# A last expert pair in a half and two quarters of its columns, and stores of whole tiles

## Chip, cores and metric

One core of one Trainium2 chip. The metric is the device time of one execution in microseconds, a median of runs; less is better. TensorE does the matmuls, VectorE and ScalarE the work on whole rows, GpSimd a few products, and SyncE (SP) issues the transfers.

## What is computed

Two layers of a transformer on 512 latent tokens of width 1024 (256 more tokens are context): layer 0 mixes by attention, layer 1 by pooling over windows of tokens. Each layer ends in a mixture of experts, 32 experts in 4 groups, two per token, and the whole in a norm:

```python
x_lat = x_lat + g_m * o_l                       # the layer's mixer
tokens = modulate(rms_norm(x_lat, norm_ffn_g[i]), sh_f, sc_f)
# per expert e and its tokens:
gu = h_pad[rows] @ w_gu[e]
y  = (silu(gu[:, :512]) * gu[:, 512:]) @ w_down[e]
f  = zeros.at[row_tok].add(y * row_w)
x_lat = x_lat + g_f * f
...
return rms_norm(x_lat, final_norm_g)
```

All of it is float32; a product that feeds the residual stream is split into a high and a low part of a shorter format and summed from both.

## The kernel before, in words

The residual stream x lies on chip as four tiles of 128 tokens by 1024 columns, `self.x(j)`, two of them side by side in each of the two tiles `self.xt`. The experts are worked through in 16 pairs: tokens of a pair are gathered by a one-hot product (line 1335), multiplied by the gate and up weights (1358), turned (1370), multiplied by the down weights (1383), weighted (1396), split into a high part on ScalarE (1397) and a low part on VectorE (1391), and scattered back to the tokens by a second one-hot product into PSUM tiles pc (1412), which VectorE adds to x (1414). The products of one pair run while the additions of the pair before are done.

The last pair of a layer has no later pair to hide its additions. `last_down` (1418) does it by halves of the 1024 columns. Each down tile holds half of the rows for 512 columns, so a half needs two tiles, `st.get()`. The order is written out by hand, and each engine works through its own instructions in the order in which they are written:

```python
products(0, 0); products(0, 1); parted(0); products(1, 0)
added(0)
after()
products(1, 1); parted(1)
...
added(1, then)
```

`products` (1431) makes a half of y in PSUM, `parted` weights and splits it (1396, 1397, 1437), `added` sums the four token tiles (1443), first all four high parts and then all four low parts, adds them to x (1446) and squares the result on ScalarE with a sum along the row (1447). From the two sums of squares comes the reciprocal root of the next norm, for two token tiles at a time (`rstd_steps`, 474 to 481): a small VectorE instruction, a root on ScalarE, and five small VectorE instructions. `after` is empty in layer 0; in layer 1 it is `gained` (1824), four products of x's first half by the final gain on GpSimd.

`last_down` is used twice. In layer 0 its norms go to the pool layer: four normed tiles xn, on VectorE, ScalarE, VectorE and GpSimd (1647, 1649), which TensorE turns (1674) and which are summed over windows; between these TensorE makes the modulation products ada_ps (354). In layer 1 the norms go to `final` (1826): ScalarE scales the first half of a token tile (1830), VectorE the second (1831), and each half is stored by its own transfer (1833).

All weights come through one stream of transfers on SP (118), in a fixed order. A tile's slot is one of 22, which the large working tiles (`self.big`, y and o among them) share; a slot is handed on when the tile's last reader is done, and `st.done()` lets the next transfer be written into the program.

Of the kernel before, what the change touches and what calls it, by code (L numbers as in the profile page):

```python
# [11 lines left out]
F32 = mybir.dt.float32  # L12
F32R = mybir.dt.float32r
BF16 = mybir.dt.bfloat16
I32 = mybir.dt.int32
AF = mybir.ActivationFunctionType
ALU = mybir.AluOpType
# [3 lines left out]
D = 1024  # L21
KD = D // 128
SEQ = 512
NT = SEQ // 128
# [154 lines left out]
class Kernel:  # L179
# [1238 lines left out]
    def last_down(self, aT, w, gf, inv, after):  # L1418


        nc, mp, pm, st = self.nc, self.mp, self.pm, self.st
        ss = [self.sm.tile([128, NT], F32, name=f"sq{h}") for h in range(2)]
        P = self.scatter(inv)
        py = [pm.tile([128, 512], F32, tag="y", name="py") for _ in range(2)]
        y = [self.big([128, 2, 512], F32R, "y") for _ in range(2)]

        def products(h, q):
            wd = st.get()
            for j in range(2):
                for e in range(2):  # L1430
                    nc.tensor.matmul(py[h][64 * e:64 * e + 64], aT[:, 2 * q + j, 64 * e:64 * e + 64], wd[:, e, j],  # L1431
                                     start=(q + j == 0), stop=(q + j == 2), tile_position=(0, 64 * e))
            st.done()

        def parted(h):
            self.gated(py[h], w, gf, h, y[h])
            nc.vector.tensor_tensor(y[h][:, 1], py[h], y[h][:, 0].bitcast(F32), op=ALU.subtract)

        def added(h, then=None):
            ps = [pm.tile([128, 512], F32, tag=t, name="pc") for t in ("c", "g", "c", "u")]  # L1440
            for part in range(2):
                for j in range(NT):
                    nc.tensor.matmul(ps[j], P[:, j * 128:(j + 1) * 128], y[h][:, part], start=(part == 0), stop=(part == 1))  # L1443
            for j in range(NT):
                xs = self.x(j)[:, h * 512:(h + 1) * 512]
                nc.vector.tensor_add(xs, xs, ps[j])  # L1446
                nc.scalar.activation(mp.tile([128, 512], F32, name="act"), xs, AF.Square, accum_out=ss[h][:, j:j + 1])  # L1447
                if then:
                    then(j)

        products(0, 0)
        products(0, 1)
        parted(0)
        products(1, 0)
        added(0)
        after()
        products(1, 1)
        parted(1)
        nc.vector.tensor_scalar(ss[0], ss[0], 1.0 / D, EPS, op0=ALU.mult, op1=ALU.add)
        r = [self.sm.tile([128, 2], F32, name=f"nr{z}") for z in range(2)]  # L1460
        steps = [self.rstd_steps(r[z], ss[1][:, 2 * z:2 * z + 2], ss[0][:, 2 * z:2 * z + 2], f"n{z}") for z in range(2)]

        def then(j):
            if j == 2:
                next(steps[0])

        added(1, then)

        def norms():

            next(steps[0])
            next(steps[1])
            for z in range(2):
                if z:
                    next(steps[1])
                for j in range(2):
                    yield 2 * z + j, r[z][:, j:j + 1]

        return norms()

    def overflow(self, i, gf):
# [344 lines left out]
    def final(self, norms):  # L1826
        nc = self.nc
        for j, r in norms:
            o = [self.big([128, 512], F32, "o") for _ in range(2)]
            nc.scalar.activation(o[0], self.xg[j], AF.Copy, scale=r)  # L1830
            nc.vector.scalar_tensor_tensor(o[1], self.x(j)[:, 512:], r, self.gn[:, 512:], op0=ALU.mult, op1=ALU.mult)  # L1831
            for h in range(2):
                nc.sync.dma_start(self.out[j * 128:(j + 1) * 128, h * 512:(h + 1) * 512], o[h])


# [36 lines left out]
```

## Time and profile before

| | before |
|---|---|
| median of 3 runs | 1404.93 us (1404.92 to 1408.68) |
| the profiled execution's own time | 1406.14 us |
| its span | 1404.2 us |
| TensorE, weight loads beside it | 94%, 53% of the span |
| VectorE, ScalarE, GpSimd | 48%, 26%, 11% |
| read from memory | 472.06 MB, 338 GB/s over the span |
| TensorE's granted clock, mean | 0.974 |

The profiler took one execution. A row gives an engine's instructions with their start and busy time; an idle time in brackets stands ahead of the instruction that ended it, with the instruction that released it. A traced float32 matmul stands for half of one in the program, so 12 of the program are 24 in the trace. Durations are sums of a stretch where rows are merged ("x4"): the end of the last less the start of the first.

### The profile page before, as it was taken

How to read it: one execution, taken by the hardware profiler on the slowest of the kernel's cores; microseconds unless marked ns; L12 is line 12 of the kernel's file. 1: busy time of each engine (PE TensorE's matmuls, PEld its weight loads, DVE VectorE, ACT ScalarE, POOL GpSimd, SP SyncE). 2: the span in 40 equal slices, each digit the busy share in tenths (PEclk: the TensorE clock that was granted, in tenths of full speed). 3: DMA queues.
4: the chain of work that ended last, by engine and by line, in shares of the span. 5: the costliest groups of instructions: out<-in, count | busy, mean ns of one | idle time of the engine just before them, and what ended most of it. 6: DMA issues, size and time to landing. Idle time of an engine off the chain costs nothing. (4 is left out here: it accounts for less than half of the span.)

```text
span 1404.2 us, 18564 instructions
## 1 busy us (share of the span) xinstructions
PE 1320.3 (94%) x7134; PEld 741.4 (53%) x7135; DVE 672.1 (48%) x1288; ACT 367.4 (26%) x707; POOL 153.7 (11%) x142
## 2 busy tenths in 40 slices
PE   4799999999799999999999997789999999999995
PEld 1588677778544544455444444654445544455432
DVE  2777788767723433243333437632433433343325
ACT  2454678753211111111111114511111111111103
POOL 1523253430000000000000014200000000000001
PEclk8899999999899999999999999889999999999998
DMA  9412845178489999999999999358999999999994
GB/s 379 153 61 65 355 152 179 52 249 325 162 344 428 426 427 426 426 427 426 426 427 426 421 418 417 127 216 366 425 428 426 427 426 427 426 426 426 427 419 155
DMA packets 80558, 475.45 MB, mean 339 GB/s; under 512 B 8496, under 2 KB 10048, under 8 KB 30288
## 3 DMA queue, kind: packets, MB, share of 16 engines
q1 hardware_dynamic: 80456, 474.19, 82.5%
q8 instruction: 59, 0.97, 0.2%
q14 instruction: 35, 0.29, 0.1%
q10 hardware_dynamic: 8, 0.01, 0.0%
HBM read 472.06 MB, written 2.11 MB: 338 GB/s over the span
## 5 line engine op out<-in xcount | busy, mean ns | idle before, releaser
L1358 PE MATMUL pgate<-wt,xe 128*64 128x512 f32 x1024 | 266.1, 597 | 4.8 <-issue 4.8
L1358 PE MATMUL pup<-wt,xe 128*64 128x512 f32 x1024 | 264.9, 594 | 0.0
L1383 PE MATMUL py<-wt,aT 128*64 128x512 f32 x960 | 212.6, 596 | 0.1
L1363 DVE TENSOR_TENSOR act<-act,pup 128x512 f32<-128x512 f32 x32 | 22.0, 687 | 336.2 <-ACT act L1362 307.0
L1414 DVE TENSOR_TENSOR x<-x,pc 128x512 f32<-128x512 f32 x240 | 154.0, 683 | 32.8 <-PE pc L1412 32.8
L1358 PEld LDWEIGHTS pgate<-wt,xe 128*64 128x64 f32 x1024 | 74.3, 138 | 147.6 <-issue 138.1
L1358 PEld LDWEIGHTS pup<-wt,xe 128*64 128x64 f32 x1024 | 75.0, 138 | 146.3 <-issue 146.3
L1335 PE MATMUL pga<-OH,xnp 128*128 128x256 f32 x960 | 135.0, 286 | 5.5 <-issue 5.5
L1412 PE MATMUL pc<-y,scat 128*128 128x512 f32 x480 | 136.6, 406 | 2.4 <-DVE x L1414 2.4
L1335 PEld LDWEIGHTS pga<-OH,xnp 128*128 128x128 f32 x960 | 127.9, 191 | 14.3 <-issue 7.3
L1396 DVE SCALAR_TENSOR_TENSOR py<-py,r_sw,gw 128x512 f32<-128x512 f32 x64 | 48.6, 759 | 177.6 <-PE py L1383 168.6
L1383 PEld LDWEIGHTS py<-wt,aT 128*64 128x64 f32 x960 | 67.0, 137 | 124.5 <-issue 117.9
L1362 ACT ACTIVATE act<-pgate 128x512 f32<-128x512 f32 x32 | 19.1, 597 | 355.2 <-PE pgate L1358 355.2
L1412 PEld LDWEIGHTS pc<-y,scat 128*128 128x128 f32 x480 | 80.5, 188 | 43.2 <-ACT act L1362 24.3
L1397 ACT ACTIVATE y<-py 128x512 fp32r<-128x512 f32 x64 | 38.2, 596 | 236.5 <-PE py L1383 183.0
L1347 ACT ACTIVATE xe<-pga,mod 128x256 f32<-128x256 f32 x64 | 35.8, 565 | 157.3 <-PE pga L1335 154.2
L545 PE MATMUL pmm<-whl,hT 128*128 128x512 f32 x288 | 70.2, 401 | 0.0
L833 DVE TENSOR_REDUCE mx<-S 128x1 f32<-128x768 f32 x64 | 58.3, 951 | 19.6 <-PE S L830 18.9
L545 PEld LDWEIGHTS pmm<-whl,hT 128*128 128x128 f32 x288 | 54.3, 192 | 11.2
L840 ACT ACTIVATE P<-S,mx 128x768 f32<-128x768 f32 x64 | 56.9, 899 | 2.2 <-POOL rest L714 2.1
L1824 POOL TENSOR_TENSOR xg<-x,gn 128x512 f32<-128x512 f32 x4 | 5.0, 1283 | 479.1 <-DVE x L1446 479.1
L850 PE MATMUL PT<-cst,P 128*128 128x128 f32 x384 | 54.5, 278 | 0.1
(341 smaller groups left out, 1433.6 us busy)
## 6 DMA issues: line engine op xcount, KB each, us to landing
wt<-in_moe_w_gate_up_dram SPq DMA_DIRECT2D x224, 1024.0 KB
wt<-in_moe_w_down_dram SPq DMA_DIRECT2D x120, 1024.0 KB
wt<-in_w_ada_dram SPq DMA_DIRECT2D x48, 1024.0 KB
wt<-in_moe_w_gate_up_dram SPq DMA_DIRECT2D x64, 512.0 KB
wt<-in_moe_w_down_dram SPq DMA_DIRECT2D x16, 512.0 KB
wt<-in_attn_w_qkv_dram SPq DMA_DIRECT2D x6, 1024.0 KB
x<-in_x_dram SPq DMA_DIRECT2D x8, 512.0 KB
wt<-in_attn_w_o_dram SPq DMA_DIRECT2D x4, 1024.0 KB
```

What stands on the lines that cost most here:

```text
L545: self.nc.tensor.matmul(p, lhs(pa, k), whl[pb, k // 4][:, k % 4], start=(k + n == 0), stop=(k == KD - 1 and n == 2))
L833: nc.vector.tensor_reduce(m, s[:, :NKEY], axis=AX, op=ALU.max, negate=True)
L840: nc.scalar.activation(P[n][:, g], S.pop((n, g))[:, :NKEY], AF.Exp, bias=mx[n, g], accum_out=total[n // 4][:, 2 * gp + g, kvl:kvl + 1])
L850: nc.tensor.transpose(pt[:, cc, g * 128:(g + 1) * 128], P[n][:, g, c * 128:(c + 1) * 128], self.ident)
L1335: nc.tensor.matmul(p[:, :n], self.parts[part][j // 2][:, j % 2, k * 128:(k + 1) * 128], OH[:, j], start=(z == 0), stop=(z == 2 * NT - 1))
L1347: nc.scalar.activation(xe, p, AF.Identity, bias=B[:, k:k + 1], scale=A[:, k:k + 1])
L1358: nc.tensor.matmul(p[64 * e:64 * e + 64], xe(k)[:, off + 64 * e:off + 64 * e + 64], w[e][:, h * 512:(h + 1) * 512], start=(k == 0), stop=( ...
L1383: nc.tensor.matmul(py[h][64 * e:64 * e + 64], aT[:, j, 64 * e:64 * e + 64], wd[e][:, h * 512:(h + 1) * 512], start=(j == 0), stop=(j == 3) ...
L1396: nc.vector.scalar_tensor_tensor(py, py, w, gf[:, h * 512:(h + 1) * 512], op0=ALU.mult, op1=ALU.mult)
L1397: nc.scalar.activation(y[:, 0], py, AF.Copy)
L1412: nc.tensor.matmul(p, P[:, j * 128:(j + 1) * 128], y[:, part], start=(part == 0), stop=(part == 1))
L1414: nc.vector.tensor_add(xs, xs, p)
```

## The change

`last_down` is done in three groups of columns: 0 to 512, 512 to 768, 768 to 1024. The down tiles are as before, so groups 1 and 2 (counted from 0) use the two halves of tiles 3 and 4, and these are given back after group 2's products. Group 1's products stand ahead of group 0's sums, and group 2's behind them. The sums of a group go token tile by token tile, high and low part one after the other. Of groups 1 and 2, two token tiles are added to x by one instruction. In the last group two of the four squares are made by VectorE. The sums of squares of the first two groups are combined ahead of the last group's. In `final` a token tile's two halves lie in one tile, and one transfer stores it.

```diff
--- before.py
+++ after.py
@@ -1419,60 +1419,107 @@
 
 
         nc, mp, pm, st = self.nc, self.mp, self.pm, self.st
-        ss = [self.sm.tile([128, NT], F32, name=f"sq{h}") for h in range(2)]
+        cols = (0, 512), (512, 768), (768, 1024)
+        ss = [self.sm.tile([128, NT], F32, name=f"sq{z}") for z in range(3)]
         P = self.scatter(inv)
-        py = [pm.tile([128, 512], F32, tag="y", name="py") for _ in range(2)]
-        y = [self.big([128, 2, 512], F32R, "y") for _ in range(2)]
-
-        def products(h, q):
-            wd = st.get()
+        py = [pm.tile([128, 512], F32, tag=t, name="py") for t in "yyt"]
+        y = [self.big([128, 2, b - a], F32R, "y") for a, b in cols]
+        wds = []
+
+        def products(z, q):
+            a, b = cols[z]
+            if z < 2:
+                wds.append(st.get())
+            wd = wds[q + 2 * (z > 0)][:, :, :, a % 512:a % 512 + b - a]
             for j in range(2):
                 for e in range(2):
-                    nc.tensor.matmul(py[h][64 * e:64 * e + 64], aT[:, 2 * q + j, 64 * e:64 * e + 64], wd[:, e, j],
+                    nc.tensor.matmul(py[z][64 * e:64 * e + 64, :b - a], aT[:, 2 * q + j, 64 * e:64 * e + 64], wd[:, e, j],
                                      start=(q + j == 0), stop=(q + j == 2), tile_position=(0, 64 * e))
-            st.done()
-
-        def parted(h):
-            self.gated(py[h], w, gf, h, y[h])
-            nc.vector.tensor_tensor(y[h][:, 1], py[h], y[h][:, 0].bitcast(F32), op=ALU.subtract)
-
-        def added(h, then=None):
-            ps = [pm.tile([128, 512], F32, tag=t, name="pc") for t in ("c", "g", "c", "u")]
+            if z != 1:
+                st.done()
+
+        def high(z):
+            a, b = cols[z]
+            p = py[z][:, :b - a]
+            nc.vector.scalar_tensor_tensor(p, p, w, gf[:, a:b], op0=ALU.mult, op1=ALU.mult)
+            nc.scalar.activation(y[z][:, 0], p, AF.Copy)
+
+        def low(z):
+            a, b = cols[z]
+            nc.vector.tensor_tensor(y[z][:, 1], py[z][:, :b - a], y[z][:, 0].bitcast(F32), op=ALU.subtract)
+
+        def sums(z, p, j):
             for part in range(2):
-                for j in range(NT):
-                    nc.tensor.matmul(ps[j], P[:, j * 128:(j + 1) * 128], y[h][:, part], start=(part == 0), stop=(part == 1))
-            for j in range(NT):
-                xs = self.x(j)[:, h * 512:(h + 1) * 512]
-                nc.vector.tensor_add(xs, xs, ps[j])
-                nc.scalar.activation(mp.tile([128, 512], F32, name="act"), xs, AF.Square, accum_out=ss[h][:, j:j + 1])
-                if then:
-                    then(j)
-
-        products(0, 0)
-        products(0, 1)
-        parted(0)
-        products(1, 0)
-        added(0)
+                nc.tensor.matmul(p, P[:, j * 128:(j + 1) * 128], y[z][:, part], start=(part == 0), stop=(part == 1))
+
+        def square(z, j, eng=None):
+            a, b = cols[z]
+            xs, o = self.x(j)[:, a:b], mp.tile([128, 512], F32, name="act")[:, :b - a]
+            if eng is nc.vector:
+                nc.vector.scalar_tensor_tensor(o, xs, 1.0, xs, op0=ALU.mult, op1=ALU.mult, accum_out=ss[z][:, j:j + 1])
+            else:
+                nc.scalar.activation(o, xs, AF.Square, accum_out=ss[z][:, j:j + 1])
+
+        def half(p, j):
+            xs = self.x(j)[:, :512]
+            nc.vector.tensor_add(xs, xs, p)
+            square(0, j)
+
+        def quarter(z, p, jj):
+
+            xs = self.xt[jj][:, :, slice(*cols[z])]
+            nc.vector.tensor_add(xs, xs, p)
+
+        for q in range(2):
+            products(0, q)
+        high(0)
+        low(0)
+        for q in range(2):
+            products(1, q)
+        high(1)
+        ps = [pm.tile([128, 512], F32, tag=t, name="pc") for t in ("c", "g", "c", "u")]
+        for j in range(NT):
+            sums(0, ps[j], j)
+        for q in range(2):
+            products(2, q)
+        half(ps[0], 0)
+        low(1)
+        for j in range(1, NT):
+            half(ps[j], j)
         after()
-        products(1, 1)
-        parted(1)
+        high(2)
+        pq = {}
+
+        def quarter_sums(z, tags):
+            for jj in range(2):
+                p = pq[z, jj] = pm.tile([128, 2, 256], F32, tag=tags[jj], name="pc")
+                for j in range(2):
+                    sums(z, p[:, j], 2 * jj + j)
+
+        quarter_sums(1, ("ga", "y"))
+        quarter(1, pq[1, 0], 0)
+        low(2)
+        quarter(1, pq[1, 1], 1)
+        quarter_sums(2, ("c", "g"))
+        for j in range(NT):
+            square(1, j)
         nc.vector.tensor_scalar(ss[0], ss[0], 1.0 / D, EPS, op0=ALU.mult, op1=ALU.add)
         r = [self.sm.tile([128, 2], F32, name=f"nr{z}") for z in range(2)]
-        steps = [self.rstd_steps(r[z], ss[1][:, 2 * z:2 * z + 2], ss[0][:, 2 * z:2 * z + 2], f"n{z}") for z in range(2)]
-
-        def then(j):
-            if j == 2:
-                next(steps[0])
-
-        added(1, then)
+        steps = []
+        for jj in range(2):
+            quarter(2, pq[2, jj], jj)
+            if jj == 0:
+                nc.vector.scalar_tensor_tensor(ss[0], ss[1], 1.0 / D, ss[0], op0=ALU.mult, op1=ALU.add)
+            square(2, 2 * jj)
+            square(2, 2 * jj + 1, nc.vector)
+            q = slice(2 * jj, 2 * jj + 2)
+            steps.append(self.rstd_steps(r[jj], ss[2][:, q], ss[0][:, q], f"n{jj}"))
+            next(steps[jj])
 
         def norms():
 
-            next(steps[0])
-            next(steps[1])
             for z in range(2):
-                if z:
-                    next(steps[1])
+                next(steps[z])
                 for j in range(2):
                     yield 2 * z + j, r[z][:, j:j + 1]
 
@@ -1826,11 +1873,10 @@
     def final(self, norms):
         nc = self.nc
         for j, r in norms:
-            o = [self.big([128, 512], F32, "o") for _ in range(2)]
-            nc.scalar.activation(o[0], self.xg[j], AF.Copy, scale=r)
-            nc.vector.scalar_tensor_tensor(o[1], self.x(j)[:, 512:], r, self.gn[:, 512:], op0=ALU.mult, op1=ALU.mult)
-            for h in range(2):
-                nc.sync.dma_start(self.out[j * 128:(j + 1) * 128, h * 512:(h + 1) * 512], o[h])
+            o = self.big([128, D], F32, "o")
+            nc.scalar.activation(o[:, :512], self.xg[j], AF.Copy, scale=r)
+            nc.vector.scalar_tensor_tensor(o[:, 512:], self.x(j)[:, 512:], r, self.gn[:, 512:], op0=ALU.mult, op1=ALU.mult)
+            nc.sync.dma_start(self.out[j * 128:(j + 1) * 128], o)
 
 
 # ---- launch: one core; inputs and outputs as the reference has them ----
```

How it moves the instructions, in either layer. On TensorE, at the end of a layer (aT is the turned activation, y the split output, scat the one-hot):

```order
 L1412 MATMUL pc<-y,scat 128x512 x4
-L1431 MATMUL py<-wt,aT 64x512 x12
-L1443 MATMUL pc<-y,scat 128x512 x8
-L1431 MATMUL py<-wt,aT 64x512 x4
-L1443 MATMUL pc<-y,scat 128x512 x8
+L1436 MATMUL py<-wt,aT 64x512 x8
+L1436 MATMUL py<-wt,aT 64x256 x8
+L1453 MATMUL pc<-y,scat 128x512 x8
+L1436 MATMUL py<-wt,aT 64x256 x8
+L1453 MATMUL pc<-y,scat 128x256 x16
```

The second half's products, four ahead of the first sums and four behind, have become eight narrower ones ahead and eight behind; the last sums are 16 of 256 columns.

On VectorE, layer 1, from the weighting of the first columns to the first reciprocal, before:

```order
L1396 SCALAR_TENSOR_TENSOR py<-py,r_sw,gw 128x512
L1437 TENSOR_TENSOR y<-py,y 128x512
L1446 TENSOR_TENSOR x<-x,pc 128x512 x4
L1396 SCALAR_TENSOR_TENSOR py<-py,r_sw,gw 128x512
L1437 TENSOR_TENSOR y<-py,y 128x512
L1459 TENSOR_SCALAR sq_10201<-sq_10201 128x4
L1446 TENSOR_TENSOR x<-x,pc 128x512 x3
L474 SCALAR_TENSOR_TENSOR n0v<-sq_10202,sq_10201 128x2
L1446 TENSOR_TENSOR x<-x,pc 128x512
L477 RECIPROCAL nr_10264<-nr_10264 128x2
```

and in the change, from the second weighting on:

```order
L1444 SCALAR_TENSOR_TENSOR py<-py,r_sw,gw 128x256
L1471 TENSOR_TENSOR x<-x,pc 128x2x256
L1449 TENSOR_TENSOR y<-py,y 128x256
L1471 TENSOR_TENSOR x<-x,pc 128x2x256
L1506 TENSOR_SCALAR sq_10232<-sq_10232 128x4
L1471 TENSOR_TENSOR x<-x,pc 128x2x256
L1512 SCALAR_TENSOR_TENSOR sq_10232<-sq_10233,sq_10232 128x4
L1459 SCALAR_TENSOR_TENSOR act,sq_10234<-x 128x256
L474 SCALAR_TENSOR_TENSOR n0v<-sq_10234,sq_10232 128x2
L1471 TENSOR_TENSOR x<-x,pc 128x2x256
L1459 SCALAR_TENSOR_TENSOR act,sq_10234<-x 128x256
L474 SCALAR_TENSOR_TENSOR n1v<-sq_10234,sq_10232 128x2
```

Low parts and additions now alternate, the update of sq stands between the last two double additions, two squares are new, and both variances come ahead of the first reciprocal. These rows begin at the third group's weighting; ahead of it stand the first group's, the second group's and the four additions of 512 columns.

On ScalarE, layer 1, from the first high part to the second root:

```order
L1445 ACTIVATE y<-py 128x512
L1445 ACTIVATE y<-py 128x256
L1461 ACTIVATE act,sq_10232<-x 128x512 x4
L1445 ACTIVATE y<-py 128x256
L1461 ACTIVATE act,sq_10233<-x 128x256 x4
L1461 ACTIVATE act,sq_10234<-x 128x256
L475 ACTIVATE nr_10339<-n0v 128x2
L1461 ACTIVATE act,sq_10234<-x 128x256
L475 ACTIVATE nr_10340<-n1v 128x2
```

The third group's high part stands behind the four squares of the first, as the second half's stood before, and four squares of the second group are new ahead of the last ones.

## Rows read from the trace of the kernel before

**Rows 1.** The table of stretches (start:end, length; then for PE, PEld, DVE, ACT and POOL the busy us and the instructions; TensorE's granted clock as a share of 2.4 GHz; share of DMA time; GB/s):

```profile
1000.00:1100.00 100.00, 100.00 (x522) 50.27 (x522) 37.10 (x62) 12.28 (x21) 0.00 (x0) 1.00 1.01 426
...
1340.00:1360.00 20.00, 19.37 (x84) 8.18 (x82) 8.32 (x13) 1.63 (x3) 0.00 (x0) 1.00 1.02 420
...
1380.00:1405.00 25.00, 10.48 (x46) 4.61 (x42) 13.51 (x30) 9.96 (x25) 4.99 (x4) 0.83 0.22 84
```

**Rows 2.** The chain of waits that ended last, in layer 1's last stretch (start us, us, engine and line it stood at):

```profile
1384.44 1.36 PE pc L1443 x5
...
1389.53 0.49 ACT y L1397
...
1395.69 0.06 DVE o L1831
```

**Rows 3.** The timeline of layer 1's last stretch (start us, busy us, engine, line, operation, shapes, count; in brackets the idle time of the engine ahead of it and what ended it):

```profile
1379.07 5.37 PE L1431 MATMUL py<-wt,aT 128*64 128x512 f32 x24
...
1382.77 0.76 DVE L1396 SCALAR_TENSOR_TENSOR py<-py,r_sw,gw 128x512 f32<-128x512 f32 x1 [2.51 <-PE py L1431]
...
1383.56 0.60 ACT L1397 ACTIVATE y<-py 128x512 fp32r<-128x512 f32 x1 [3.37 <-DVE py L1396]
1384.19 0.69 DVE L1437 TENSOR_TENSOR y<-py,y 128x512 fp32r<-128x512 f32 x1 [0.66 <-ACT y L1397]
...
1384.37 2.11 PE L1443 MATMUL pc<-y,scat 128*128 128x512 f32 x8
1385.83 2.48 DVE L1446 TENSOR_TENSOR x<-x,pc 128x512 f32<-128x512 f32 x4 [0.94 <-PE pc L1443]
...
1386.55 0.63 ACT L1447 ACTIVATE act<-x 128x512 f32<-128x512 f32 x1 [2.39 <-DVE x L1446]
1386.65 4.99 POOL L1824 TENSOR_TENSOR xg<-x,gn 128x512 f32<-128x512 f32 x4 [479.10 <-DVE x L1446]
...
1387.30 0.63 ACT L1447 ACTIVATE act<-x 128x512 f32<-128x512 f32 x1
...
1392.35 0.63 ACT L1447 ACTIVATE act<-x 128x512 f32<-128x512 f32 x1 [2.33 <-DVE x L1446]
...
1394.70 0.17 DVE L477 RECIPROCAL nr<-nr 128x2 f32<-128x2 f32 x1
...
1396.66 4.05 SPq L1833 DMA_DIRECT2D out_dram<-o  x8
```

**Rows 4.** The timeline of layer 0's last stretch and of the pool layer's beginning (columns as in rows 3):

```profile
835.07 5.37 PE L1431 MATMUL py<-wt,aT 128*64 128x512 f32 x24
...
850.70 0.17 DVE L477 RECIPROCAL nr<-nr 128x2 f32<-128x2 f32 x1
...
852.58 0.33 PE L1674 MATMUL pt<-cst,xn 128*128 128x128 f32 x1 [3.37 <-DVE xn L1649]
...
855.22 3.89 PE L1674 MATMUL pt<-cst,xn 128*128 128x128 f32 x17 [0.51 <-POOL xn L1649]
...
859.03 2.67 PE L354 MATMUL ada_ps<-wt,cond 128*32 128x512 f32 x16
...
865.19 1.04 PE L1674 MATMUL pt<-cst,xn 128*128 128x128 f32 x8
...
866.16 1.92 PE L354 MATMUL ada_ps<-wt,cond 128*32 128x512 f32 x16
```

**Rows 5.** The table of stretches for the last us (columns as in rows 1):

```profile
1397.00:1398.00 1.00, 0.00 (x0) 0.00 (x0) 0.83 (x6) 0.24 (x1) 0.00 (x0) 0.50 0.49 193
...
1400.00:1401.00 1.00, 0.00 (x0) 0.00 (x0) 0.00 (x0) 0.00 (x0) 0.00 (x0) 0.50 1.07 410
...
1402.00:1403.00 1.00, 0.00 (x0) 0.00 (x0) 0.00 (x0) 0.00 (x0) 0.00 (x0) 0.50 0.74 283
```

**Rows 6.** Instructions grouped by line and shape, on VectorE and ScalarE (count | busy us in all, mean ns of one | idle us ahead):

```profile
L698 DVE TENSOR_TENSOR q<-pmm,h4r 128x256 f32<-128x256 f32 x6 | 2.5, 424 | 0.3
...
L598 DVE SCALAR_TENSOR_TENSOR xn<-xc 128x1024 f32<-128x1024 f32 x1 | 1.2, 1217 | 0.0
...
L1722 ACT ACTIVATE act<-x 128x256 f32<-128x256 f32 x16 | 6.7, 417 | 10.2 <-DVE x L1719 9.9
```

**Rows 7.** TensorE's timeline in the middle of layer 1, where sums of 512 columns and gathers of 256 take turns (columns as in rows 3):

```profile
1001.21 1.11 PE L1335 MATMUL pga<-OH,xnp 128*128 128x256 f32 x8
1002.16 1.10 PE L1412 MATMUL pc<-y,scat 128*128 128x512 f32 x4
```

**Rows 8.** The timeline of SP's queue: the last down tiles of either layer (start of the first issue, us to the end of the last, count):

```profile
818.72 9.39 SPq L118 DMA_DIRECT2D wt<-in_moe_w_down_dram  x8
...
1359.95 9.29 SPq L118 DMA_DIRECT2D wt<-in_moe_w_down_dram  x8
```

**Rows 9.** The instructions of the tile sq, and those of line 1688, on VectorE (count: least/median/most ns, first and last start us; shapes):

```profile
L1459 DVE TENSOR_SCALAR sq<-sq x2: 159/582/1006, 846.7 to 1390.7; 128x4 f32<-128x4 f32 x2
...
L1688 DVE TENSOR_TENSOR pab<-pab x6: 723/1488/1495, 861.5 to 879.6; 128x541 f32<-128x541 f32 x3, 128x537 f32<-128x537 f32 x2, 128x529 f32<-128x529 f32 x1
```

**Rows 10.** The table of stretches around the clock's fall and rise in the pool layer, and after the last weights (columns as in rows 1):

```profile
854.00:856.00 2.00, 1.26 (x5) 0.97 (x6) 0.18 (x1) 0.27 (x1) 1.53 (x9) 0.50 1.05 438
...
860.00:862.00 2.00, 2.00 (x18) 0.55 (x11) 1.93 (x5) 0.78 (x1) 1.06 (x3) 0.85 1.04 424
...
1378.00:1380.00 2.00, 2.00 (x10) 0.76 (x11) 1.77 (x4) 1.89 (x3) 0.00 (x0) 1.00 0.05 17
```

## Prediction

> **What bounds the kernel now.** I read the table by stage first: between 1000 and 1100 us TensorE is busy for the whole stretch at clock 1.00, after 1380 for 10.48 of 25 us [rows 1]; the change sits at the two places where TensorE stands still, this one and the start of the pool layer. Then the chain of waits for the last 25 us: it hops from TensorE to ScalarE, VectorE and back, so there latency counts and no engine's sum does [rows 2]. Then the timeline of that stretch, which gives each duration and start [rows 3], and the same stretch of layer 0 [rows 4]. Call T the start of the first down product: 1379.07 in layer 1, 835.07 in layer 0. In both layers the half order runs alike: the reciprocal that follows the last sum of squares starts at 1394.70 and at 850.70, which is T + 15.63 twice. So I work out one time, that of the reciprocal.
>
> The last piece, after the norm, is bound by the stores: the first is issued at 1396.66, bytes flow at 401 to 410 GB/s from some 1397.5 to 1402.7, and the span ends at 1404.2 [rows 3, 5]. Stores end a fixed time after the first one starts, not after the last output.
>
> **The chain as it will be, from T.** The first half's products stay: VectorE starts its weighting at T + 3.70, ScalarE copies the high part until T + 5.09, the low part is ready at T + 5.81 (1384.19 + 0.69) [rows 3].
>
> - Second group's products (256 columns) move ahead of the additions: 16 traced matmuls. At 512 columns 24 take 5.15 us (5.37 less the tail that overlaps the next), 0.215 each [rows 3]. At 256 I bound one from below at half, 0.107, and from above at no saving, 0.215. The nearest row is the gather, also 256 columns: where the eight of one turn go by in 0.95 us, 0.119 each [rows 7]. I take 0.113: 1.8 us, done at T + 5.24, under the wait for the low part, so it costs nothing.
> - The additions now go by token tile, high then low, so their second matmul waits for the low part: T + 6.00 (0.2 from VectorE to TensorE, as between 1384.16 and 1384.36). The first sum reaches VectorE 0.61 later (the fifth matmul of the eight began near 1385.22, the add at 1385.83 [rows 3]): T + 6.61, against T + 6.76 before. The eight end at T + 7.49, and the third group's products at T + 9.30.
> - VectorE: add 0 until T + 7.30, low part of group 2 (0.42, from 0.424 for 256 columns [rows 6]), adds 1 to 3 at a pitch of 0.61 until T + 9.49, then the third group's weighting. It needs products that end at T + 9.30 plus 0.27 and runs from T + 9.57 for 0.49 (0.76 at 512 less 256 columns' worth, 0.27).
> - ScalarE carries four squares at a pitch of 0.75 [rows 3] from T + 7.34, held once by add 1, and only then the copy of group 3's high part: T + 10.45 to 10.85. Group 2's first double addition ends at T + 10.8; the low part at T + 11.3; the second double addition at T + 11.95. Group 3's sums wait for that low part and reach VectorE at T + 12.35 (0.2, three matmuls of 0.119, 0.49).
> - Group 2's four squares on ScalarE take 0.54 each (0.417 and what of the accumulator's read does not overlap, as 0.63 stands for 0.75 above [rows 3, 6]); the last two wait for the second double addition and end at T + 13.1. The update of the partial sums waits for them. **This, not the matmuls, is the late one.**
> - From there: a square on VectorE (0.5, an estimate: 1024 columns with an accumulated sum took 1.217, so 256 take 0.8 less, and its accumulator is read after it [rows 6]) beside one on ScalarE, the first variance near T + 13.85, the last double addition until T + 14.6, two squares until T + 15.2, the second variance, the reciprocal at **T + 15.4**, 0.23 earlier than now.
>
> Added work that is covered: VectorE gets 1.5 us more in small instructions (two weightings of 0.49 for one of 0.76, two low parts of 0.42 for one of 0.69, two squares, one update), ScalarE 0.4; they fill the idle time that stands before them now, 0.94 before the first add and 2.39 and 2.33 before ScalarE's squares [rows 3]. Without that cover the 1.5 us would be a loss.
>
> **Layer 0** gets the 0.23 only if the pool layer hands it on. There TensorE idles 3.37 us until the first normed tile at 852.58 and turns them all only from 855.22 [rows 4], so it follows the norm. SP's queue: group 2 takes the third and fourth down tile at T + 3.4 and 4.3, where the fourth was needed at T + 7.34. In layer 1 the stream has run dry by 1378, T - 1 (17 GB/s from 1378 to 1380) [rows 10]; in layer 0 its issue starts at T - 16.35 against T - 19.12 [rows 8], so the fourth lands near T + 1.8, 2.5 us ahead. The third group's y takes one more slot for a moment and the slots of tiles 3 and 4 come free at T + 9.3 instead of some 1 to 2 us earlier; the transfers behind them are gate and up weights that layer 1 uses only after the pool layer. Cost nothing; gain **0.23**.
>
> [...] GpSimd multiplies the four x halves from 1386.65 on for 4.99 us, and VectorE's 128x4 tensor_scalar on sq took 1.006 us there, 0.159 in layer 0 where GpSimd is idle [rows 3, 9]. Started at 1390.7, it ended with GpSimd (1386.65 + 4.99 = 1391.64). In the new order the first x half is ready at T + 7.30, so GpSimd ends at T + 12.45; the same instruction stands at T + 11.9 and would end at T + 12.5, which puts the sums of group 3 0.15 later; ScalarE's squares hide half of it. Gain **0.15**.
> [...]
>
> **Stores.** Four of 512 KB for eight of 256 KB. The first went out at 1396.66, when ScalarE's half was ready; VectorE's began at 1395.69 [rows 2] and takes some 0.76, as a weighting of the same size does, so it was ready first and waiting for both halves adds nothing. Tile 3 is ready at about 1399.3, while tiles 0 to 2 still flow until 1401. The rows double to 4 KB: no gain at the low end, and at the other the 420 GB/s of the 4 KB rows of weights between 1340 and 1360 [rows 1], where 2.1 MB take 5.0 us for 5.2. The middle: **0.12**.
>
> **Sum:** 0.23 + 0.15 + 0.12 = 0.5 us. The profiled execution took 1406.14 (span 1404.2), 1.2 above the median of 1404.93, so it would read 1405.6; against the median I forecast **1404.4**.
>
> **Rivals.**
> - *No gain: the third group is as late as the second half was.* A split instruction costs more in these rows: 2 x 0.424 against 0.69 is 0.16 for each [rows 3, 6]. ScalarE's queue (four squares, copy, four squares) or small-instruction latency takes back the 0.4. For: ScalarE has no slack from T + 7.3 to 13.1 by my count. Against: it idles 2.33 us before its last squares now [rows 3]. Time 1404.9 to 1405.0. [...]
> - *Slower: products of 256 columns do not halve.* The place is the third group's products, which gate its weighting. At 0.119 they add 0.1; every 0.01 more costs 0.16 per layer, so from 0.13 on nothing is gained. At 0.175, above the middle of the two bounds (if weight loads are no longer hidden), the layers lose 0.77 and 0.85, less the stores: 1406.4; with no saving, 1407.7. Against: the gather's 0.119 at the same width, with twice the weight columns to load [rows 7].
> - *The clock moves.* In the pool layer the granted clock is 0.50, the 1.2 GHz level, from about 854 to 860.6, after TensorE stood idle, and returns some 5 us after dense work resumes [rows 4, 10]. Denser work ahead of it could shift that. Sixteen ada matmuls take 2.67 us in it and 1.92 outside [rows 4], 17 transposes 3.89 against 2.2 (8 in 1.04): at most 2.4 us back, 1402.0, or, with 3 us more of it, 1.5 lost: 1405.9.
> - [...] If GpSimd ends 1 us later, the tensor_scalar and all behind it move by 0.8: 1405.1.
>
> **Chances.** Forecast 0.42; no gain 0.2; slow products 0.1; clock better 0.1, worse 0.08; port 0.07; 0.03 is left for things I don't see, such as a late weight tile. About 0.3% (4.2 us) is what a measurement of this kernel can tell from no change: the three runs span 3.8 us. No case but the remainder and the far end of the clock or the products reaches it: faster 0.03, same 0.93, slower 0.04. The range, 1402.0 to 1406.5, takes in the clock to its better end, and the products at 0.175.
>
> **What would show it.** Right: reciprocals near T + 15.4, group 3's high copy near T + 10.5 behind four squares, ScalarE busy without a gap to T + 13, the tensor_scalar on sq still over 0.4 us in layer 1, four stores at 405 to 420 GB/s. Wrong: a gap at the third group's weighting, waiting for products; the reciprocal later than T + 15.7; low clock ending elsewhere than near 860.

## The result

| | median, us | lowest to highest | ratio to before (95% interval) |
|---|---|---|---|
| before | 1407.97 | 1404.92 to 1408.68 (6 runs) | |
| the change | **1419.33** | 1418.60 to 1420.66 (6 runs) | 1.0088 (1.0075 to 1.0101) |
| forecast | 1404.4 | 1402.0 to 1406.5 | |

The kernel became 0.9% slower, some 12 us, where half a microsecond less was forecast. (The six runs of before hold the three of the table ahead and three beside the change; two lie near 1405 and four near 1408. The forecast took its 0.5 us off 1404.93, the median of the first three; off the six it would have been 1407.5.) The profiled execution took 1420.66 us, its span is 1418.5: 14.3 more than the 1404.2 of before.

**Where the 14.3 us are.** Two starts cut each layer: T, at which the last pair's first down product starts, and the first reciprocal behind it. The first two columns are their times:

| | before | after | added in this piece |
|---|---|---|---|
| start to T, layer 0 | 835.07 | 842.62 | 7.55 |
| T to the reciprocal, layer 0 | 850.70 | 858.85 | 0.60 |
| from there to T, layer 1 | 1379.07 | 1392.78 | 5.56 |
| T to the reciprocal, layer 1 | 1394.70 | 1409.02 | 0.61 |
| from there to the end of the span | 1404.2 | 1418.5 | -0.02 |

Before T of layer 0 both programs have the same instructions, and still 7.55 us are lost there. So 13.1 of the 14.3 us lie where the change did nothing, and 1.2 where it did something. The two have different causes.

Not all of the 13.1 can be put down to one thing. The first gate product of layer 0 starts at 382.40 for 381.14, 1.26 later, and from the reciprocal to the first gate product of layer 1 it is 79.23 us for 77.39, 1.84 more. Kernels that are as fast as before differ by more in both: 380.45 to 382.36, and 76.15 to 78.76. What is left is the work on the experts, from the first gate product to T: 460.22 us for 453.93 in layer 0 and 454.70 for 450.98 in layer 1, 6.29 and 3.72 more, **10.0 in all**.

**The stream is slower, in the whole program.** The table of stretches of the change (columns as in [rows 1]), of the middle of either layer and of the end:

```profile
420.00:820.00 400.00, 399.32 (x2018) 192.36 (x2016) 146.24 (x246) 47.99 (x82) 7.47 (x6) 1.00 1.01 420
1000.00:1100.00 100.00, 100.00 (x515) 49.23 (x512) 35.29 (x59) 11.74 (x20) 0.00 (x0) 1.00 1.01 421
1340.00:1360.00 20.00, 19.69 (x88) 6.67 (x84) 4.89 (x8) 1.79 (x3) 0.00 (x0) 1.00 1.01 420
1393.00:1418.00 25.00, 11.88 (x72) 6.57 (x68) 14.80 (x38) 11.18 (x31) 5.01 (x4) 0.80 0.25 99
```

and the first stretch before:

```profile
420.00:820.00 400.00, 399.28 (x2028) 192.68 (x2026) 147.49 (x248) 48.16 (x82) 7.47 (x6) 1.00 1.01 426
```

Read the last two numbers: the DMA engines are busy all the time in both, 1.01, but move 420 GB/s for 426, and 421 between 1000 and 1100 for the 426 of [rows 1]. TensorE looks the same, busy 399.3 of 400 us at clock 1.00, and that is the trap: matmuls are counted busy while they are spread out behind their weights (e2 below shows it: 1330.5 us busy for 1320.3 with the same instructions). The count of instructions hints at it, 2018 for 2028 in the same 400 us, 515 for 522 in the second stretch. The whole span in 40 slices, before:

```profile
GB/s 379 153 61 65 355 152 179 52 249 325 162 344 428 426 427 426 426 427 426 426 427 426 421 418 417 127 216 366 425 428 426 427 426 427 426 426 426 427 419 155
```

and after:

```profile
GB/s 367 160 60 64 352 157 171 51 273 321 164 349 421 421 421 420 422 421 420 421 420 421 412 406 411 117 210 362 420 421 420 421 420 422 420 421 421 420 413 172
```

Twenty slices of 35.1 us stand near 426.5 before and near 420.7 after: 702 us, of which 1.4% is 9.7 us. The three at 421 to 417 fall to 412 to 406, 2.2% of 105 us, 2.3 more, and the one before the last 0.5. That is 12.5 us of the stream's own time, of which the 10.0 above arrive at T. **This stream is busy all the time and hardly ahead of the engine that it feeds: of the 12.5 us that it loses in rate, the program loses 10.0 in time.**

Where TensorE feels it is seen among its weight loads. Their idle time from 100 to 1400 us that a landing of gate and up weights ended (us, times), before:

```profile
DMA wt<-in_moe_w_gate_up_dram: 3.4, 11
```

and after:

```profile
DMA wt<-in_moe_w_gate_up_dram: 12.9, 24
```

9.5 us more, nearly the 10.0. The longest waits come at the last gate and up tiles of layer 0, after:

```profile
827.20 0.13 PEld L1358 LDWEIGHTS pgate<-wt,xe 128*64 128x64 f32 x1 [1.09 <-DMA wt<-in_moe_w_gate_up_dram]
...
829.76 0.13 PEld L1358 LDWEIGHTS pgate<-wt,xe 128*64 128x64 f32 x1 [1.09 <-DMA wt<-in_moe_w_gate_up_dram]
...
832.32 0.13 PEld L1358 LDWEIGHTS pgate<-wt,xe 128*64 128x64 f32 x1 [1.08 <-DMA wt<-in_moe_w_gate_up_dram]
...
834.88 0.13 PEld L1358 LDWEIGHTS pgate<-wt,xe 128*64 128x64 f32 x1 [1.09 <-DMA wt<-in_moe_w_gate_up_dram]
```

One such wait per tile of 1 MB, 2.56 us apart: 410 GB/s, so TensorE eats tiles as they land (a shorter wait, 0.23 or 0.24 us, stands between each two). Before, the last of these tiles came with 0.17 us of waiting, so the margin there was already used up:

```profile
827.33 0.19 PEld L1358 LDWEIGHTS pgate<-wt,xe 128*64 128x64 f32 x2 [0.17 <-DMA wt<-in_moe_w_gate_up_dram]
```

**The last pair, 0.6 later instead of 0.23 sooner.** The timeline of layer 1's last stretch after the change (columns as in [rows 3]):

```profile
1392.78 5.38 PE L1436 MATMUL py<-wt,aT 128*64 128x512 f32 x32
...
1399.19 0.69 DVE L1465 TENSOR_TENSOR x<-x,pc 128x512 f32<-128x512 f32 x1 [0.19 <-PE pc L1453]
...
1400.47 1.95 PE L1436 MATMUL py<-wt,aT 128*64 128x256 f32 x16
...
1402.46 0.49 DVE L1444 SCALAR_TENSOR_TENSOR py<-py,r_sw,gw 128x256 f32<-128x256 f32 x1 [0.47 <-PE py L1436]
...
1404.66 0.33 DVE L1506 TENSOR_SCALAR sq<-sq 128x4 f32<-128x4 f32 x1
1404.90 0.67 DVE L1471 TENSOR_TENSOR x<-x,pc 128x512 f32<-128x512 f32 x1
...
1406.07 0.42 ACT L1461 ACTIVATE act<-x 128x256 f32<-128x256 f32 x1
1406.07 0.16 DVE L1512 SCALAR_TENSOR_TENSOR sq<-sq,sq 128x4 f32<-128x4 f32 x1 [0.49 <-ACT act L1461]
1406.61 0.42 DVE L1459 SCALAR_TENSOR_TENSOR act<-x 128x256 f32<-128x256 f32 x1 [0.38 <-ACT act L1461]
...
1407.93 0.42 ACT L1461 ACTIVATE act<-x 128x256 f32<-128x256 f32 x1 [0.45 <-DVE x L1471]
1408.47 0.42 DVE L1459 SCALAR_TENSOR_TENSOR act<-x 128x256 f32<-128x256 f32 x1 [0.64 <-ACT act L1461]
...
1409.02 0.16 DVE L477 RECIPROCAL nr<-nr 128x2 f32<-128x2 f32 x1
...
1410.83 3.31 SPq L1879 DMA_DIRECT2D out_dram<-o  x4
```

Take T = 1392.78 off each start. As far as the update of sq (1406.07, T + 13.29) the steps stand where the forecast had them, to a quarter of a us. Then look at the brackets of the two squares on VectorE: 0.38 and 0.64 us of idle time that end with ScalarE's square of line 1461. Both engines write their squares into the scratch tile act, of which there is one, and so they take turns where they were to run side by side.

### The profile page after: what moved, and what is told of

Its sections match the earlier page's. It is cut to its first block, busy times and chain, and to the rows that moved or that the text cites. A ratio compares the mean times of both kernels' runs of the same rounds, so it can differ in the third digit from the quotient of the medians.

```text
span 1418.5 us, 18682 instructions
## 1 busy us (share of the span) xinstructions
PE 1331.5 (94%) x7182; PEld 747.2 (53%) x7183; DVE 673.5 (47%) x1302; ACT 368.7 (26%) x717; POOL 153.6 (11%) x142
## 5 line engine op out<-in xcount | busy, mean ns | idle before, releaser
L1358 PE MATMUL pgate<-wt,xe 128*64 128x512 f32 x1024 | 281.4, 597 | 5.8 <-issue 5.0
L1358 PE MATMUL pup<-wt,xe 128*64 128x512 f32 x1024 | 279.1, 594 | 0.0
L1358 PEld LDWEIGHTS pgate<-wt,xe 128*64 128x64 f32 x1024 | 77.5, 137 | 156.0 <-issue 136.4
L1358 PEld LDWEIGHTS pup<-wt,xe 128*64 128x64 f32 x1024 | 78.5, 137 | 146.6 <-issue 146.3
L1396 DVE SCALAR_TENSOR_TENSOR py<-py,r_sw,gw 128x512 f32<-128x512 f32 x60 | 45.5, 758 | 172.4 <-PE py L1383 168.7
```

Source lines behind the costliest of these rows:

```text
L1358: nc.tensor.matmul(p[64 * e:64 * e + 64], xe(k)[:, off + 64 * e:off + 64 * e + 64], w[e][:, h * 512:(h + 1) * 512], start=(k == 0), stop=( ...
L1396: nc.vector.scalar_tensor_tensor(py, py, w, gf[:, h * 512:(h + 1) * 512], op0=ALU.mult, op1=ALU.mult)
```

## Experiments

Each ratio is against runs of the kernel before on the same chip. "Base" is the byte of a partition at which the 22 slots of the large tiles (weights, y, o) begin. A slot has 8192 bytes, so all slots stand alike to a multiple of 256. The new third tile `sq2` takes two buffers of 32 bytes in the pool of small tiles, which lies ahead of the slots, and the layout of the compiled programs shows the base at 30208 = 118 x 256 before and at 30272 after the change.

**1. Base or order?** In the first four runs theory A is the base, B the new order of the work, C chance.

e1_change_base_kept: the change, with `sq1` and `sq2` in one buffer each, so that the base is 30208 again.

```diff
-        ss = [self.sm.tile([128, NT], F32, name=f"sq{z}") for z in range(3)]
+        ss = [self.sm.tile([128, NT], F32, name=f"sq{z}", bufs=(2, 1, 1)[z]) for z in range(3)]
```

> The whole change, but the 32 bytes per buffer of its third sum of squares are taken from the second buffers of the other two, so that the pool of large tiles begins at byte 30208 of each partition as before, and not at 30272. Theory A (the weight stream is slower because the tiles it writes have moved by 64 bytes, to a base that is no longer a multiple of 512): the stream is back at 426 GB/s in the middle of the layers, the last products of layer 0 start near 835 instead of 842.6, and the time is that of before plus the 0.6 us that each last pair lost by itself (T + 16.24 for T + 15.63): 1.2 us over before, ratio 1.001. Theory B (the new order of the last pair, its later release of two weight slots or its extra y slot slows the stream): 421 GB/s and 1419 us as with the change, ratio 1.008 to 1.009. Theory C (chance of the chip or of the program's size): 1419 us as well.

e2, e3 and e4 are the kernel before with one unused tile among the small ones, of 8, 16 or 32 elements in two buffers: the base moves by 64, 128 or 256 bytes, and with it the small tiles ahead of the slots and the working tiles behind them; no instruction changes.

```diff
             es.enter_context(tc.manual_schedule())
+            self.pad = self.sm.tile([128, 8], F32, name="pad")
```

> The kernel before, with an unused tile of 2 x 32 bytes in the small pool, so that every large tile begins 64 bytes higher, at 30272, as in the change. Nothing else is touched. Theory A: 420 to 421 GB/s in the middle of the layers, layer 0's last products start 7.5 us later, layer 1's 13 us later; the change's time less its 1.2 us in the two last pairs, ratio to before 1.007 to 1.008. Theories B and C: the time of before, ratio 1.000.

> The kernel before with every large tile 128 bytes higher (base 30336, a multiple of 128 and not of 256). Theory A leaves open which step counts: if multiples of 64 are bad and of 128 are good, 426 GB/s and the time of before; if it takes 256 or 512, 421 GB/s and a ratio of 1.007 to 1.008. Theories B and C: the time of before.

> The kernel before with every large tile 256 bytes higher (base 30464, a multiple of 256 and not of 512). Theory A: 426 GB/s and the time of before if 256 is enough; 421 GB/s and a ratio of 1.007 to 1.008 if the rate needs multiples of 512. Theories B and C: the time of before.

**2. Which distance?** e9 (8 elements, one buffer) and e10 (24 elements, two) move the base by 32 and 192 bytes; e7 is the change as it is with 24 elements in two buffers, so that its base stands 256 above the old one.

> The kernel before with 32 bytes of unused tile ahead of the large ones: they begin 32 bytes above their old place. Theory P (a transfer costs the bytes between the 256-byte boundary and its start, so 32 is half of 64): the stream at 424 to 425 GB/s and 2 to 6 us more, ratio 1.002 to 1.004. Theory Q (any place off the boundary costs one piece more for each row, however far off): 420 to 421 GB/s as at 64 and 128 bytes, ratio 1.006 to 1.010.

> The same with 192 bytes. Theory P: three times the bytes of 64, the stream at 412 to 417 GB/s, 20 us more or beyond, ratio above 1.012. Theory Q: 420 to 421 GB/s, ratio 1.006 to 1.010.

> The change as it is (third tile with two buffers) with 192 bytes of unused tile more, so that the large tiles begin 256 bytes above their old place in place of 64. Theory A (the place off a multiple of 256 bytes slows the weight stream): 425 to 428 GB/s, T back near 836 and 1381, ratio 0.999 to 1.002. Rival (the second buffer of the third tile, or the change itself, costs the 13 us): ratio 1.007 to 1.010, as the change.

All of them, with the rate from 1000 to 1100 us in the profiled execution:

| kernel | base moved by | GB/s | T, layer 0 | T, layer 1 | median, us | ratio (95% interval) |
|---|---|---|---|---|---|---|
| the change | 64 | 421 | 842.62 | 1392.78 | 1419.33 | 1.0088 (1.0075 to 1.0101) |
| e1 the change | 0 | 426 | 836.51 | 1382.48 | 1407.33 | 1.0002 (0.9993 to 1.0012) |
| e7 the change | 256 | 426 | 834.27 | 1377.64 | 1405.81 | 0.9993 (0.9982 to 1.0005) |
| e9 before | 32 | 419 | 845.47 | 1394.95 | 1419.36 | 1.0093 (1.0076 to 1.0109) |
| e2 before | 64 | 421 | 844.29 | 1392.54 | 1418.79 | 1.0076 (1.0062 to 1.0090) |
| e3 before | 128 | 421 | 843.44 | 1391.60 | 1416.75 | 1.0066 (1.0051 to 1.0081) |
| e10 before | 192 | 421 | 842.50 | 1390.77 | 1417.07 | 1.0078 (1.0060 to 1.0097) |
| e4 before | 256 | 426 | 836.51 | 1379.51 | 1407.48 | 0.9997 (0.9988 to 1.0007) |

The stretch from 1000 to 1100 of e3:

```profile
1000.00:1100.00 100.00, 100.00 (x517) 49.95 (x514) 36.03 (x60) 12.09 (x21) 0.00 (x0) 1.00 1.01 421
```

and of e4, which is moved twice as far:

```profile
1000.00:1100.00 100.00, 100.00 (x523) 50.52 (x522) 37.08 (x63) 12.28 (x21) 0.00 (x0) 1.00 1.01 426
```

Theory A holds in both directions: an unused tile makes the kernel before as slow as the change, and the change with the base at a multiple of 256 is as fast as the kernel before. B falls with e2 (old order, slow), C with the eight rows together.

Two readings of the traces leave the pool layer and its clock out (they take in e5, e6 and e8 below, whose base is that of before). From the first gate product to T, layer 1 takes 450.97 to 450.98 us in the seven kernels whose base is a multiple of 256, and 454.70 to 455.82 in the five others; layer 0 453.72 to 456.27 and 460.20 to 463.85. And from 1000 to 1100 us a packet of 8192 bytes takes 309.4 to 309.5 ns on average in the seven, 313.9 to 315.0 in the five: the transfer itself is longer. That in layer 1 the seven agree to 0.01 us says that TensorE sets the pace there at 426 GB/s, and only just.

The other tiles that move, those of the engines, cost nothing that shows: VectorE's 240 additions to x take 683 ns on average in before, in e2 and in e9, and the gate products 597 in all three. For the same instructions TensorE is counted busy 1330.5 us in e2 and 1320.3 before.

Of the distances, theory P (the loss grows with the bytes beyond the boundary) falls: 32 bytes cost no less than 64, and 192 no more. Q's rate stands, a loss that is there or not, 1.6% at 32 bytes and 1.2% at 64 to 192; at 32 bytes the rate is a little lower still, 419. That a piece more for each row is its cause was the author's guess and is not shown. In e2, e3, e4, e9 and e10 the sources of the transfers stay and the destinations move.

**3. Why the last pair is late.** In the next two, C is the shared scratch tile, D the latency of small instructions and of VectorE beside a busy GpSimd, where the tensor_scalar on sq took 1.006 us for 0.159 [rows 9] ("the port" of the expectation is the author's name for this; its cause is not shown). e5_own_scratch is e1 with VectorE's squares written into a tile that is free by then:

```diff
-            xs, o = self.x(j)[:, a:b], mp.tile([128, 512], F32, name="act")[:, :b - a]
+            xs = self.x(j)[:, a:b]
             if eng is nc.vector:
+                o = mp.tile([128, 4, 128], F32, name="aT").rearrange("p a b -> p (a b)")[:, :b - a]
                 nc.vector.scalar_tensor_tensor(o, xs, 1.0, xs, op0=ALU.mult, op1=ALU.mult, accum_out=ss[z][:, j:j + 1])
             else:
+                o = mp.tile([128, 512], F32, name="act")[:, :b - a]
```

> The change with the other tiles back in their old place, and VectorE's squares writing into a tile of their own. Theory C (the squares ran one after the other because VectorE's and ScalarE's write the same scratch tile): VectorE's squares no longer wait for ScalarE's; the first reciprocal stands near T + 15.4, 0.8 earlier than T + 16.23, in both layers; some 1.7 us less than the change with its base kept, ratio to the kernel before 0.9985 to 1.0000. Rival D (the latency of small instructions and the port set it): the reciprocal stays at T + 16.0 or later, and the ratio at 1.0002.

e8_squares_on_scalare is e1 with all squares on ScalarE:

```diff
-            square(2, 2 * jj + 1, nc.vector)
+            square(2, 2 * jj + 1)
```

> The change with its base kept and the last group's four squares all on ScalarE. Theory C (VectorE's and ScalarE's squares take turns on one scratch tile anyway): four in a row on ScalarE end no later than two and two in turns; the reciprocal at T + 15.9 to 16.4. Rival D (they run side by side, and latency elsewhere sets T + 16.23): two squares more on ScalarE put it at T + 16.8 to 17.4.

The end of layer 1's last pair in e5:

```profile
1382.81 5.38 PE L1436 MATMUL py<-wt,aT 128*64 128x512 f32 x32
...
1396.09 0.42 ACT L1463 ACTIVATE act<-x 128x256 f32<-128x256 f32 x1
1396.09 0.16 DVE L1514 SCALAR_TENSOR_TENSOR sq<-sq,sq 128x4 f32<-128x4 f32 x1 [0.49 <-ACT act L1463]
1396.17 0.42 DVE L1460 SCALAR_TENSOR_TENSOR aT<-x 128x256 f32<-128x256 f32 x1
...
1397.50 0.43 DVE L1460 SCALAR_TENSOR_TENSOR aT<-x 128x256 f32<-128x256 f32 x1
1397.56 0.42 ACT L1463 ACTIVATE act<-x 128x256 f32<-128x256 f32 x1 [0.46 <-DVE x L1473]
...
1398.18 0.16 DVE L477 RECIPROCAL nr<-nr 128x2 f32<-128x2 f32 x1
```

and in e8:

```profile
1379.86 5.38 PE L1436 MATMUL py<-wt,aT 128*64 128x512 f32 x32
...
1395.08 0.42 ACT L1461 ACTIVATE act<-x 128x256 f32<-128x256 f32 x1 [0.45 <-DVE x L1471]
...
1395.62 0.42 ACT L1461 ACTIVATE act<-x 128x256 f32<-128x256 f32 x1
...
1396.24 0.16 DVE L477 RECIPROCAL nr<-nr 128x2 f32<-128x2 f32 x1
```

The reciprocal stands in e1 at T + 16.23 in both layers, in e5 at T + 15.38 (853.82 less 838.44) and T + 15.37 (1398.18 less 1382.81), in e8 at T + 16.38 in both. In e5 the squares of the two engines start 0.08 and 0.06 us apart and none waits for the other. Four squares on ScalarE cost 0.15 more than two and two in turns, so the turns had left next to nothing of the second engine. C holds, D falls. As times, e5 has 1406.16 us, ratio 0.9991 (0.9979 to 1.0003), and e8, run once, 1407.73: the 0.85 us per layer are beyond what medians can tell here, so the offsets from T decide.

**4. Whole-tile stores alone.** e6_whole_tile_stores is the kernel before with the new `final` and nothing else.

> The kernel before with whole-tile stores alone, all tiles in their old place. Forecast on record: 0.12 us less; from the first store's issue to the end 7.42 us for 7.54, and the first issue no later after the reciprocal (1396.66 - 1394.70 = 1.96). Rival: the transfers of 4 KB rows flow no faster and the first has to wait for VectorE's half, so 0 to 0.6 us more. Ratio 0.9995 to 1.0005 by both, so the profile's offsets decide.

The stretches of its end (columns as in [rows 5]):

```profile
1398.00:1400.00 2.00, 0.00 (x0) 0.00 (x0) 0.08 (x1) 0.05 (x1) 0.00 (x0) 0.50 0.97 397
...
1400.00:1401.00 1.00, 0.00 (x0) 0.00 (x0) 0.00 (x0) 0.00 (x0) 0.00 (x0) 0.50 1.02 422
```

1407.35 us, ratio 1.0001 (0.9990 to 1.0012). The first store is issued 1.95 us after the first reciprocal (1.96 before), and the end follows 7.58 us later (1402.9 less 1395.32), for 7.54. The rate does rise, 422 GB/s for the 410 of [rows 5], but between 1398 and 1400 it is 397. No gain: the 0.04 lost is less than the 0.1 to which a span is given.

## Why the prediction was wrong

**The step that failed** is the claim that what the change adds beside the path costs nothing. Its words were "Cost nothing; gain 0.23", said of queue and slots in layer 0. It counted every instruction, and followed a slot's time, but not its place. The diff's second line makes three tiles of two, 64 bytes; they moved every large tile off a multiple of 256 bytes, and the stream, which [rows 1] showed at 426 GB/s with its engines busy all the time, fell to 421. No rival held this, and the 0.03 left for "things I don't see, such as a late weight tile" was its only room. What the rows did hold was the exposure: with the stream as full as in [rows 1], over 24 slices of 35.1 us, each per cent of its rate is worth up to 8.4 us, more than fifteen times the gain that the forecast worked out. A change against such a stream has to be asked first what it does to the stream.

**The second, mis-sized**, is the end of the chain: "a square on VectorE ... beside one on ScalarE", the reciprocal at T + 15.4. It came at T + 16.24 and 16.23. The work was sized well; that the two shared one scratch tile stood in `square`, and the rows of the order in front named act as the target on both engines. With a tile of its own (e5) it is T + 15.38 and 15.37.

The rest of the chain held, the stores apart:
- Products of 256 columns halve: 16 take 1.95 us, and eight of 512 columns take 1.94 before. The rival of products that do not halve falls. So does that of no gain: with e5's scratch tile the reciprocal is earlier than before, T + 15.37 for T + 15.63, so the split instructions fit into idle time.
- The first addition came at T + 6.41 (1399.19), forecast 6.61; the third group's weighting at T + 9.68 (1402.46), forecast 9.57; the update at T + 13.29, forecast just after 13.1.
- VectorE beside GpSimd, in the chances "port": no run shows a port. What shows is that layer 1's tensor_scalar on sq ends as GpSimd does, at 1391.67 for 1391.64 before and at 1404.99 for 1404.96 in the change. There it began at T + 11.88 (1404.66), forecast 11.9, and took 0.33 us where 0.6 was forecast, and 0.16 in layer 0. In e5 both layers have the same offset to 0.01, so this costs the reciprocal nothing in the new order, and layer 1 gains 0.26 there where 0.15 was forecast. VectorE's new squares come after it: in the trace of the change GpSimd ends at T + 12.18 (1404.96) and the first of them starts at T + 13.83.
- The stores did not: forecast 0.12 gained (the middle of its 0 and 0.2 is 0.1), measured 0.04 lost (e6).

With base and scratch set right, T to the end of the span is 24.79 us in e5 (1407.6 less 1382.81) for 25.13 before, 0.34 less, with spans given to 0.1: the forecast for layer 1, the reciprocal and the stores together, was 0.27. In layer 0 the reciprocal is 0.25 sooner, but whether the pool layer hands that on can't be seen, for the reason in the last section. So by these offsets the idea was worth about what was forecast, which no median here can tell from nothing, and what came with it cost more than twenty times as much.

e5 and e7 are the fastest forms of the change, and the intervals of both include the kernel before.

## What to carry to other kernels

Before costing a change's instructions, list the tiles that it adds, also the smallest, and see which pools lie behind theirs: if transfers fill a tile, keep its start where it was or, by the runs here, at a multiple of 256 bytes (426 GB/s there, 419 to 421 off it), and look at the rate of the stream in a stretch that the change does not touch. Where a stream is busy all the time and hardly ahead, expect most of what its rate loses to be the kernel's loss (here 10.0 of 12.5 us), whatever the chain of waits says of the last microseconds. When a step is given to a second engine to run beside the first, look for what both write: here a scratch result that nobody reads made them take turns, and the reciprocal 0.85 us later.

## What the runs showed that was not expected

**The start of the destination matters, not its distance.** 32, 64, 128 and 192 bytes off a multiple of 256 all bring the stream from 426 to between 419 and 421 GB/s at the same busy share of 1.01; 256 bytes bring no loss. What happens inside the DMA engines no row shows. Nor do the runs tell weights from the other large tiles, since all slots move together, and the tiles behind them too; the weights are nearly all of the bytes.

**The clock dips a second time in the pool layer in some executions and not in others.** One burst of 16 products, in e1:

```profile
879.28 5.38 PE L1755 MATMUL pp<-pw,pab 128*128 128x256 f32 x16 [2.01 <-DVE pab L1745]
```

and in e7, which from the last pair to there has the same instructions:

```profile
877.04 3.86 PE L1756 MATMUL pp<-pw,pab 128*128 128x256 f32 x16 [2.00 <-DVE pab L1746]
```

Both follow an idle time of 2 us. The granted clock under the first is 0.50:

```profile
880.00:882.00 2.00, 2.00 (x6) 1.60 (x6) 1.97 (x4) 1.51 (x6) 0.00 (x0) 0.50 0.99 418
```

and under the second 1.00:

```profile
878.00:880.00 2.00, 2.00 (x11) 1.77 (x10) 1.97 (x4) 1.72 (x7) 0.00 (x0) 1.00 1.02 430
```

That is 1.5 us. The traces of the change, of e2, e3, e9 and e10 have the long burst, those of e4, e6 and e8 the short one, and the kernel before, whose pool layer is that of e6, the long one at 5.41. In e5 the bursts fall differently. From the first reciprocal of layer 0 to the first gate product of layer 1 it is 78.76 us in e1 and 76.15 in e7; 1 us more of this comes from the gather ahead of that product, which begins at clock 0.50 in both and takes 10.58 us in e1 and 9.63 in e7. So the rival "the clock moves" goes on without the change, by more than the 0.23 us that the change was to hand on there. These are different programs with one trace each; but two executions of before alone, on the chip of e5 to e8, took 1403.74 us at a mean clock of 0.978 and 1410.42 at 0.971. That all five kernels off a multiple of 256 have the long burst is not explained.
